# Reading the moving operand of the split products in pairs of columns from its two halves, in a one-core hybrid encoder layer

## The chip, the cores and the metric

The kernel runs on one NeuronCore of one Trainium2 chip. The metric is the device time of one execution in microseconds. A kernel is timed in several runs, and the median is given.

## The reference

One layer of a bidirectional encoder, on 1024 tokens of width 1024, in float32, followed by a final RMSNorm:

```
h = rmsnorm(x)
q, k, v, r, lr_f, lr_b, u, g_a, g_b = split(h @ w_in)
# branch A: gated linear attention, forward and backward, 4 heads, decays from lr_f and lr_b
o = gla(q, k, v, decay_f) + flipped gla(q, k, v, decay_b)
o = rmsnorm_per_head(o) * gla_norm * silu(r)
y_a = o @ w_branch_gla
# branch B: centred means over windows 2, 4, 8, 16, minus the token, a linear map per group
y_b = pooled(u) @ w_pool_group * pool_scale
x = x + (sigmoid(g_a) * y_a + sigmoid(g_b) * y_b) @ w_out
gate, up = split(rmsnorm(x) @ w_ffn_in)
x = x + (silu(gate) * up) @ w_ffn_out
return rmsnorm(x)
```

The feed-forward width is 2816. Nearly all of the arithmetic is in matrix products of float32 data.

## The kernel before

**The split products.** A float32 matrix is held as two parts of the type fp32r: the high part, a rounded copy that ScalarE makes (`split_to`, line 200), and the low part, the difference, that VectorE or GpSimd makes (line 201). A product of two such matrices is three matmuls into the same PSUM bank, high by high, high by low and low by high. `products` (line 270) issues them, at line 273. `mm3` (line 275) calls it and then `pump`, which advances a list of side tasks (splits, loads, evictions) by the cost of the product just issued, and so sets the order in which the other engines' instructions stand among the matmuls.

**A matmul** takes a stationary operand (128 rows by 128 columns, loaded into the array by a weight load of its own, LDWEIGHTS in the profile, on a row called PEld) and a moving operand (128 rows by up to 512 columns, in SBUF), and adds the result into a bank of 512 columns in PSUM. Each of the three matmuls of a product has a weight load of its own. Most split products move 512 columns. Those of the attention (tiles `kv` and `op`, 264 matmuls) move 256, the width of a head's values. All of them read neighbouring columns one after the other, and write them so.

**The stages.** The first norm and the projections of queries, keys, values and the gates r; the chunked attention of four heads, whose steps are interleaved with those projections; gates and pooling; the branch projection, the merge and the output projection; the second norm; the feed-forward product in, in 22 units of 128 rows of each half; and the product out. The large products from the gates on are done with Strassen's scheme in Winograd's form, seven products of half size with sums before and after. Sums and split weights that are needed later are stored to DRAM and loaded again.

**Four more places** issue matmuls of fp32r operands: `low_rank` (line 547), whose weights hold high and low parts side by side; the decays' map from rank 16 (line 822); and the identity products that add a residual into a bank at the end (line 2100). `products` is the fourth, through `mm3`, and directly for the attention's states (tile `kv`) and outputs (tile `op`). The scores (line 929), the products of queries with states (line 998) and all transposes work on plain fp32, and are not among them.

**What reads the banks.** ScalarE and VectorE read whole banks, or their first 256 columns, in the ordinary order, when the last matmul into them is done. Eight banks of PSUM are shared between two pools of three and five.

Of the kernel before, what the change touches and what calls it, by code (L numbers as in the profile page):

```python
# [53 lines left out]
def kernel(  # L54
# [20 lines left out]
    nc = tc.nc  # L75
# [21 lines left out]
    def slot(dtype=F32, shape=(2, HALF), s="slot"):  # L97
        return slots.tile([P, *shape], dtype, tag="slot", name=name(s))

    def t2(width=HALF, dtype=F32, s="t"):  # L100
        return tmp.tile([P, width], dtype, tag="t2", name=name(s), padded_shape=[P, HALF + 2 * PAD])
# [7 lines left out]
    def bank(pool, s="ps"):  # L109
        return pool.tile([P, HALF], F32, tag=pool.name, name=name(s))  # L110

    def as_f32(ap):
        return ap.bitcast(F32)
# [43 lines left out]
    def settle():  # L157
        while put_off:
            put_off.pop(0)[1]()

    def pump(dt):
        for entry in put_off:
            entry[0] -= dt
        while put_off and put_off[0][0] <= 0:
            put_off.pop(0)[1]()
        if pending:
            credit[0] += dt
            if credit[0] >= 2:
                credit[0] = 0.0
                pending.pop(0)()  # L170
        if aside:
            aside[0][1] -= dt

            if aside[0][1] <= 0 and not pending:
                cost = next(aside[0][0], None)
                if cost is None:
                    aside.pop(0)
                else:
                    aside[0][1] += cost
        if not side:  # L180
            return
        side[0][1] -= dt
        while side and side[0][1] <= 0:
            try:
                side[0][1] += next(side[0][0])
            except StopIteration:
                side.pop(0)
# [11 lines left out]
    def split_to(hi, lo, src, eng=nc.vector):  # L199
        nc.scalar.copy(hi, src)  # L200
        eng.tensor_tensor(lo, src, as_f32(hi), op=ALU.subtract)  # L201
# [65 lines left out]

    mm_banks = cycle([ps_mm])

    def products(ps, a, b, first=True, last=True, onto=False):  # L270

        for n, (i, j) in enumerate(((0, 0), (0, 1), (1, 0))):
            nc.tensor.matmul(ps, a[i], b[j], start=first and n == 0, stop=last and n == 2, skip_group_check=onto)  # L273

    def mm3(ps, a, b, first, last, onto=False):
        products(ps, a, b, first, last, onto)
# [19 lines left out]
    def feature_major(w, act, half, kts=KT):  # L296
        ps = bank(next(mm_banks))
        for k in range(kts):
            mm3(ps[:, :], w(k), act(k, half), k == 0, k == kts - 1)
        return ps  # L300
# [121 lines left out]
    up = slot(F32R, (HEADS, 2, DK), "up")  # L422
# [118 lines left out]
    lrT = slot(F32R, (2, HALF), "lrT")  # L541

    def low_rank(half):
        ps = bank(ps_mm)
        for k in range(KT):
            for i in range(2):
                nc.tensor.matmul(
                    ps[:, :], lw[k // 4][:, k % 4, :, :].rearrange("p a r -> p (a r)"), hT(k, half)[i],
                    start=k == 0 and i == 0, stop=k == KT - 1 and i == 1,
                )  # L550
            pump(2 / 3)
        nc.scalar.copy(lrT[:, half, :], ps[:, :])
        nc.vector.tensor_tensor(lrT[64:96, half, :], ps[64:96, :], as_f32(lrT[64:96, half, :]), op=ALU.subtract)
# [259 lines left out]
    def attention(h):  # L813
# [5 lines left out]
        zs, las = {}, {}  # L819
        for half, d in runs:  # L820
            z = bank(ps_g, "z")
            nc.tensor.matmul(z[:, :], up[:, h, d, :], lrT[:, half, :], start=True, stop=True)
            bias = b_dec[d][:, h : h + 1]
            la = t2(s="la")
            nc.vector.tensor_scalar(la[:, :], z[:, :], bias, 0.0, op0=ALU.add, op1=ALU.min)
            nc.scalar.activation(z[:, :], z[:, :], AF.Abs, bias=bias)
            zs[half, d] = z
            las[half, d] = la
            yield 1.3
# [94 lines left out]
        def scores(half):  # L924
            sc = [bank(ps_g, "sc") for _ in range(2)]
            for d in range(2):
                for i in range(4):
                    n = 4 * half + i
                    nc.tensor.matmul(
                        sc[d][:, i * CH : (i + 1) * CH], chunk_of(ke, n, d), chunk_of(qe, n, d),  # L930
                        start=True, stop=True,
                    )
            hi, lo = (t2(dtype=F32R, s="p")[:, :] for _ in range(2))
            nc.vector.copy_predicated(sc[1][:, :], keep.rearrange("p n c -> p (n c)"), sc[0][:, :])
            split_to(hi, lo, sc[1][:, :])
            return hi, lo
# [30 lines left out]
        for n in range(NT - 1, 0, -1):  # L967
            m = n - 1
# [9 lines left out]
        p = scores(0)  # L978
# [6 lines left out]
        for n in range(NT):  # L985
            half, i = n // 4, n % 4
# [22 lines left out]
            if n == 3:  # L1009
                p = q_next  # L1010
# [201 lines left out]
    for j in range(KT - 2):  # L1212
# [10 lines left out]
        for half in range(2):  # L1223
# [5 lines left out]
            ps = feature_major(w, hT, half)  # L1229
# [292 lines left out]
    for n, run in enumerate(gate_runs):  # L1522
        zs[n] = Gates(n)
        last = n == len(gate_units) - 1
# [387 lines left out]
    def load_piece():  # L1912
        if len(loaded_pieces) == len(pieces):
            return
        p, q, c = pieces[len(loaded_pieces)]
        g, w = slot(s="gor"), slot(s="wor")
        if p in RAW_B:
            i, j = RAW_B[p]
            src = w_ffn_out[(i * PAIRS + q) * P : (i * PAIRS + q + c) * P, j * HALF : (j + 1) * HALF]
            nc.sync.dma_start(w[:, :c, :], src.rearrange("(q p) c -> p q c", p=P))  # L1920
        else:
            nc.sync.dma_start(w[:, :c, :], t_out[p][:, q : q + c, :])
        nc.sync.dma_start(g[:, :c, :], g_out[p][:, q : q + c, :])
        loaded_pieces.append((w, g))

    def split_piece():
        n = len(ready_pieces)
        if n == len(pieces):
            return
        while len(loaded_pieces) <= n:  # L1930
            load_piece()
        c = pieces[n][2]
        both = []
        for src, eng in zip(loaded_pieces[n], (nc.vector, nc.gpsimd)):
            hi, lo = slot(F32R, s="oh"), slot(F32R, s="ol")
            split_to(hi[:, :c, :], lo[:, :c, :], src[:, :c, :], eng)
            both.append((hi, lo))
        ready_pieces.append(both)
# [42 lines left out]
    def load_x2():  # L1981
        t = len(x2)
        if t == NT:
            nc.sync.dma_start(gain_final[:, :], norm_final[None, :].broadcast_to([P, D]))
            return
        x2.append(slot(shape=(D,), s="x2"))
        nc.sync.dma_start(x2[t][:, :], x2_out[t])
# [76 lines left out]
    for at, p in enumerate(OUT_ORDER):  # L2064
        closing = at == len(OUT_ORDER) - 1
        if p in FIRST:
            banks[p in UP] = [bank(pool) for pool in (U_BANKS if p == 1 else X_BANKS)]
        sums = banks[p in UP]
        if closing:
            res, unit_matrix = slot(F32R, s="res"), slot(F32R, s="unit")[:, 0, :P]  # L2070
            residual = res[:, 0, :], res[:, 1, :]
            nc.scalar.copy(unit_matrix, ident[:, :])
            split_to(*residual, x2[NT - 1][:, COLS[0]])
        for i in range(CLOSE if closing else n_of):
            n = at * n_of + i
            while len(ready_pieces) <= n:
                split_piece()
            load_piece()
            if n < NT + 1:
                load_x2()  # L2080
            for m in range(4):
                piece_product(sums[m], n, m, i == 0 and p in FIRST, i == n_of - 1, p not in FIRST)
                if i == n_of - 1:
                    collect(p, m, sums[m][:, :])
                if m == (3 if i == n_of - 1 else 1):
                    split_piece()

                if m == 3 and n in (9, 10):
                    load_piece()
                    if n == 10:  # L2090
                        split_piece()
                if m == 3 and len(pieces) - n_of + CLOSE > n + 1 >= len(pieces) - 2 * CLOSE:
                    load_piece()
                    split_piece()
        if closing:
            settle()
            for m in range(4):
                if m == 3:
                    for part in residual:
                        nc.tensor.matmul(sums[m][:, :], unit_matrix, part, start=False, stop=False, skip_group_check=True)  # L2100
                for i in range(CLOSE, n_of):
                    piece_product(sums[m], at * n_of + i, m, False, i == n_of - 1, p not in FIRST)
                collect(p, m, sums[m][:, :])
# [29 lines left out]
```

## Time and profile before

| | us |
|---|---|
| median of 3 runs | 1374.78 |
| lowest and highest run | 1374.72, 1375.25 |
| profiled execution, first to last instruction (span) | 1373.4 |
| TensorE matmuls busy | 1361.4 |
| TensorE weight loads busy | 1132.9 |
| VectorE busy | 836.8 |
| GpSimd busy | 752.1 |
| ScalarE busy | 647.3 |

The span is that of one profiled execution, and the median that of the timed runs. They differ by 1.4 us, which is what lies around the first and the last instruction. Busy times are unions, so matmuls that overlap count once. The length of a single matmul in the profile reaches from its start to the end of its drain, and the next one starts before that end; how many fit into a stretch is read from the starts. Weight loads run beside the matmuls, on a row of their own (PEld). The granted clock of TensorE, as a mean over the span, was 0.999 of full speed.

### The profile page before, as it was taken

Reading aid. Unit: us, or ns where it says so; the run is one execution under the profiler, and the core shown is the slowest. Engines: PE = TensorE matmul, PEld = TensorE weight load, DVE = VectorE, ACT = ScalarE, POOL = GpSimd, SP = SyncE. Lnnn points to the kernel's source line nnn. Section 1 sums busy time; section 2 is a strip of 40 time slices with the busy share of each in tenths; the row PEclk is TensorE's granted clock in tenths of the full one; section 3 lists DMA queues with packets and bytes.
Section 4 is the critical chain, followed back from the end, with each engine's and each line's share of the span. In section 5 each row is a group of like instructions: output and inputs, shape, how many; then the busy total and the mean of one; then the engine's idle time right before and its main releaser. Section 6 shows DMA issues by size and latency. Waiting matters only on the chain. (4 is left out here: it accounts for less than half of the span.)

```text
span 1373.4 us, 17879 instructions
## 1 busy us (share of the span) xinstructions
PE 1361.4 (99%) x6310; PEld 1132.9 (82%) x6310; DVE 836.8 (61%) x1034; ACT 647.3 (47%) x1177; POOL 752.1 (55%) x557
## 2 busy tenths in 40 slices
PE   9999999999999999999999999999999999999998
PEld 7888888888888888888888888888888888888886
DVE  6974556554735777678883955655566556343375
ACT  7365666755534445554346533333333334444253
POOL 3323723222597547667764376666676667455454
PEclk9999999999999999999999999999999999999999
DMA  6321523314778569995416355555544447985451
GB/s 227 113 87 52 181 90 92 95 60 123 245 236 278 186 198 308 373 386 216 150 71 241 112 174 176 176 176 177 176 145 137 146 136 266 384 301 187 169 215 77
DMA packets 167834, 251.97 MB, mean 183 GB/s; under 512 B 11160, under 2 KB 94144, under 8 KB 167744
## 3 DMA queue, kind: packets, MB, share of 16 engines
q1 hardware_dynamic: 167600, 250.57, 53.8%
q8 instruction: 49, 0.80, 0.2%
q14 instruction: 41, 0.34, 0.1%
q10 hardware_dynamic: 144, 0.26, 0.0%
HBM read 168.74 MB, written 82.05 MB: 183 GB/s over the span
## 5 line engine op out<-in xcount | busy, mean ns | idle before, releaser
L201 POOL TENSOR_TENSOR wl<-fs,wh 128x512 fp32r<-128x512 f32 x124 | 173.1, 1400 | 163.5 <-ACT wh L200 104.0
L273 PE MATMUL ps<-gh,wh 128*128 128x512 f32 x616 | 240.5, 390 | 0.0
L273 PE MATMUL ps<-gl,wh 128*128 128x512 f32 x616 | 239.8, 389 | 0.3 <-DVE gl L1691 0.3
L273 PE MATMUL ps<-gh,wl 128*128 128x512 f32 x616 | 239.7, 389 | 0.0
L201 POOL TENSOR_TENSOR wl<-fraw,wh 128x512 fp32r<-128x512 f32 x93 | 134.0, 1442 | 75.0 <-ACT wh L200 72.4
L201 POOL TENSOR_TENSOR ol<-gor,oh 128x1024 fp32r<-128x1024 f32 (+1 forms) x42 | 101.3, 2417 | 86.0 <-ACT oh L200 71.7
L273 PE MATMUL ps<-hh,wh 128*128 128x512 f32 x356 | 145.1, 408 | 0.7 <-ACT ga L1474 0.7
L273 PE MATMUL ps<-hh,wl 128*128 128x512 f32 x356 | 139.0, 390 | 0.0
L273 PE MATMUL ps<-hl,wh 128*128 128x512 f32 x356 | 138.8, 390 | 0.0
L273 PEld LDWEIGHTS ps<-gl,wh 128*128 128x128 f32 x616 | 115.7, 188 | 24.5 <-DVE gl L1691 0.7
L273 PEld LDWEIGHTS ps<-gh,wh 128*128 128x128 f32 x616 | 115.7, 188 | 24.1 <-ACT hb L1710 0.2
L273 PEld LDWEIGHTS ps<-gh,wl 128*128 128x128 f32 x616 | 115.7, 188 | 23.9
L273 PE MATMUL ps<-oh,oh 128*128 128x512 f32 x308 | 119.8, 389 | 0.0
L273 PE MATMUL ps<-ol,oh 128*128 128x512 f32 x308 | 119.8, 389 | 0.0
L273 PE MATMUL ps<-oh,ol 128*128 128x512 f32 x308 | 119.8, 389 | 0.0
L201 POOL TENSOR_TENSOR wl<-wraw,wh 128x512 fp32r<-128x512 f32 x56 | 92.3, 1679 | 44.7 <-ACT wh L200 44.6
L201 POOL TENSOR_TENSOR wl<-raw,wh 128x512 fp32r<-128x512 f32 x34 | 47.4, 1404 | 108.3 <-ACT wh L200 71.9
L201 DVE TENSOR_TENSOR ol<-wor,oh 128x1024 fp32r<-128x1024 f32 (+1 forms) x42 | 62.8, 1506 | 68.1 <-ACT oh L200 55.5
L200 ACT CAST wh<-fs 128x512 fp32r<-128x512 f32 x124 | 76.1, 615 | 29.5 <-DVE fs L1093 28.3
L273 PEld LDWEIGHTS ps<-hh,wl 128*128 128x128 f32 x356 | 66.8, 188 | 14.4
L273 PEld LDWEIGHTS ps<-hh,wh 128*128 128x128 f32 x356 | 67.0, 188 | 13.1 <-ACT ga L1474 1.1
L273 PEld LDWEIGHTS ps<-hl,wh 128*128 128x128 f32 x356 | 67.0, 188 | 12.0
(281 smaller groups left out, 3073.4 us busy)
## 6 DMA issues: line engine op xcount, KB each, us to landing
fraw<-in_w_ffn_in_dram SPq DMA_DIRECT2D x44, 512.0 KB, 6.1
gor<-g_out SPq DMA_DIRECT2D x35, 512.0 KB, 6.1
fraw<-in_w_in_dram SPq DMA_DIRECT2D x22, 512.0 KB, 6.5
g_out<-s SPq DMA_DIRECT2D x44, 256.0 KB, 2.3
wor<-t_out SPq DMA_DIRECT2D x20, 512.0 KB, 3.7
raw<-in_w_in_dram SPq DMA_DIRECT2D x36, 256.0 KB, 5.1
g_out<-g SPq DMA_DIRECT2D x33, 256.0 KB, 2.6
x<-in_x_dram SPq DMA_DIRECT2D x16, 512.0 KB, 5.6
```

Of the source, the lines that this page charges most:

```text
L200: nc.scalar.copy(hi, src)
L201: eng.tensor_tensor(lo, src, as_f32(hi), op=ALU.subtract)
L273: nc.tensor.matmul(ps, a[i], b[j], start=first and n == 0, stop=last and n == 2, skip_group_check=onto)
```

## The change

Two helpers are added. `woven` takes an access pattern of `2 * 2 * c` columns as two halves, and walks through it in runs of two: columns 0 and 1 of the first half, columns 0 and 1 of the second, columns 2 and 3 of the first, and so on. `multiply` issues a matmul whose moving operand and whose output in PSUM are both walked through in that order. Every column still meets the same weights and ends at the same place of the bank. The stationary operand is passed as before. All matmuls of fp32r operands are issued through `multiply`; those of plain fp32 and the transposes stay as they were.

```
+    def woven(ap):
+
+        return ap.rearrange("p (a c e) -> p c a e", a=2, e=2)
+
+    def multiply(ps, a, b, **flags):
+        nc.tensor.matmul(woven(ps), a, woven(b), **flags)
+
     def products(ps, a, b, first=True, last=True, onto=False):
 
         for n, (i, j) in enumerate(((0, 0), (0, 1), (1, 0))):
-            nc.tensor.matmul(ps, a[i], b[j], start=first and n == 0, stop=last and n == 2, skip_group_check=onto)
+            multiply(ps, a[i], b[j], start=first and n == 0, stop=last and n == 2, skip_group_check=onto)
...
         for k in range(KT):
             for i in range(2):
-                nc.tensor.matmul(
+                multiply(
                     ps[:, :], lw[k // 4][:, k % 4, :, :].rearrange("p a r -> p (a r)"), hT(k, half)[i],
                     start=k == 0 and i == 0, stop=k == KT - 1 and i == 1,
                 )
...
             z = bank(ps_g, "z")
-            nc.tensor.matmul(z[:, :], up[:, h, d, :], lrT[:, half, :], start=True, stop=True)
+            multiply(z[:, :], up[:, h, d, :], lrT[:, half, :], start=True, stop=True)
...
                     for part in residual:
-                        nc.tensor.matmul(sums[m][:, :], unit_matrix, part, start=False, stop=False, skip_group_check=True)
+                        multiply(sums[m][:, :], unit_matrix, part, start=False, stop=False, skip_group_check=True)
```

## The prediction

> **What bounds the kernel now.** I read the page first: the engines' busy times, then the granted clock.
>
> ```profile
> span 1373.4 us, 17879 instructions
> PE 1361.4 (99%) x6310; PEld 1132.9 (82%) x6310; DVE 836.8 (61%) x1034; ACT 647.3 (47%) x1177; POOL 752.1 (55%) x557
> PEclk9999999999999999999999999999999999999999
> ```
>
> PE is busy for 99% of the span, nothing else is above 61% apart from its own weight loads, and the clock is granted nearly in full, so there is no throttle to lift or to fall into. Busy matmuls overlap, so I next read the chain of waits and the stretch that it names:
>
> ```profile
> 761.27 601.99 PE ps L273 x2654
> ```
>
> ```profile
> 761.00:1363.00 602.00, 601.73 (x2654) 498.27 (x2655) 339.45 (x327) 233.57 (x368) 366.72 (x234) 1.00 0.55 186
> ```
>
> The first row is one unbroken run on the path: 2654 products of line 273 in 601.99 us, 0.2268 us each. The second, busy time by stage (PE, PEld, DVE, ACT, POOL, then clock, DMA share, GB/s), says that in that stretch PE was idle for 0.3 us of 602. So the time is the number of matmuls times the spacing of their starts. The mean of about 389 ns that the groups show for one matmul includes its drain, which overlaps the next; the price is the spacing. It does not come from other traffic:
>
> ```profile
> 500.00:600.00 100.00, 100.00 (x441) 1.00 0.96 341
> ...
> 1000.00:1100.00 100.00, 100.00 (x443) 1.00 0.46 149
> ```
>
> With the DMA engines 96% busy or 46% busy, 100 us hold the same number of matmuls within two.
>
> **What the change touches.** It adds and removes no instruction, no wait, no tile, no DMA. It changes the order in which a product of fp32r operands reads its moving operand and writes its bank: columns 0, 1, 256, 257, 2, 3, 258, 259 and so on, for 512 columns. The stationary operand, loaded by its own instruction, is still read in order. How many products are touched is counted from the stage and group views:
>
> ```profile
> 0.00:1374.00 1374.00, 1313.74 (x5736) 1061.41 (x5736) 1.00 0.54 183
> ```
>
> ```profile
> L273 PE MATMUL kv<-vh,kt 128*128 128x256 f32 x112 | 33.7, 323 | 0.0
> ...
> L273 PE MATMUL op<-vh,p 128*128 128x256 f32 x64 | 17.1, 288 | 0.7 <-DVE p L201 0.4 <-ACT p L200 0.3
> ...
> L273 PE MATMUL kv<-vl,kt 128*128 128x256 f32 x56 | 15.7, 281 | 0.0
> ...
> L273 PE MATMUL op<-vl,p 128*128 128x256 f32 x32 | 9.0, 280 | 0.0
> L547 PE MATMUL ps<-hh,lw 128*128 128x512 f32 x16 | 6.4, 401 | 0.0
> ...
> L547 PE MATMUL ps<-hl,lw 128*128 128x512 f32 x16 | 6.3, 391 | 0.0
> L822 PE MATMUL z<-lrT,up 128*128 128x512 f32 x16 | 6.2, 390 | 0.0
> ...
> L2100 PE MATMUL ps<-res,unit 128*128 128x512 f32 x2 | 0.6, 389 | 0.0
> ```
>
> The first row is line 273 alone: 5736 matmuls. Of these 112 + 64 + 56 + 32 = 264 have 256 columns, so 5472 have 512. With 16 + 16 + 16 + 2 = 50 more from the other lines, 5522 matmuls of 512 columns and 264 of 256 are rewoven. The plain fp32 products and the transposes are not touched.
>
> **Where the spacing comes from.** Three stretches of the timeline (start, length, engine, line, what). First the settled case, then one around the attention's small products:
>
> ```profile
> 900.01 0.39 PE L273 MATMUL ps<-gh,wh 128*128 128x512 f32 x1
> ...
> 906.81 0.39 PE L273 MATMUL ps<-gh,wh 128*128 128x512 f32 x1
> ```
>
> ```profile
> 128.27 0.28 PE L273 MATMUL op<-vh,p 128*128 128x256 f32 x1
> 128.39 0.28 PE L273 MATMUL op<-vl,p 128*128 128x256 f32 x1
> 128.50 0.28 PE L273 MATMUL op<-vh,p 128*128 128x256 f32 x1
> 128.62 0.59 PE L998 MATMUL op<-sf,qe 128*128 128x256 f32 x2
> 128.87 0.58 PE L273 MATMUL ps<-hh,wh 128*128 128x512 f32 x1
> 129.28 0.39 PE L273 MATMUL ps<-hl,wh 128*128 128x512 f32 x1
> ...
> 131.59 0.39 PE L273 MATMUL ps<-hh,wh 128*128 128x512 f32 x1
> ```
>
> ```profile
> 900.01 0.19 PEld L273 LDWEIGHTS ps<-gl,wh 128*128 128x128 f32 x1
> 900.24 0.19 PEld L273 LDWEIGHTS ps<-gh,wl 128*128 128x128 f32 x1
> ```
>
> From 900.01 to 906.81 lie 30 spacings (the same product comes round after three): 6.80 / 30 = 0.2267 us for 512 columns. From 128.27 to 128.62 lie three of 256 columns: 0.35 / 3 = 0.117 us. The second 256 columns therefore cost 0.2267 - 0.117 = 0.110 us, which makes 0.219 us for 512 at the marginal rate and leaves a part of about 8 ns that every matmul pays whatever its width. From 129.28 to 131.59 ten spacings take 2.31 us, 0.231 each: after plain fp32 work has upset the rhythm, the same matmul takes 4 ns longer, then settles again. So the surplus is no constant fee; it depends on timing between two streams. The last fence shows which two I suspect: the next weight load starts together with each matmul and reads its 128 columns (0.19 us) while the matmul streams. The two L998 rows with the first product behind them take 129.28 - 128.62 = 0.66 us; less 0.231 for that product, each plain fp32 matmul takes 0.215 us for its 256 columns, with a weight load beside it as well. That is 0.84 ns per column, half the rate, so the moving stream asks for half as much.
>
> The Trainium skill speaks here, both ways. "TensorE: Matmul & The Clock Gate", section "Back-to-back issue gap", gives a 512-column matmul 215.8 ns at full clock; the rows above show 226.7, so about 11 ns here are above its figure, and a matmul brought down to it would make the estimate 1374.8 - 5522 x 0.0109 = 1315 us. The same page, "Step-by-step: what each phase is for", says that a weight load does not steal read bandwidth from the running matmul, since the two have ports of their own. By that rule my suspicion falls, and with it the gain: the time would be that of my first rival. The trace shows a surplus that comes once per matmul, and cannot show its cause.
>
> **The sum for the forecast.** I take the surplus to be collisions between the matmul's reads and the weight load's. Reading in order, the matmul walks through 512 / 0.227 = 2.26 columns per ns and the weight load through 128 / 0.19 = 0.67, so the one passes the other's place again and again. Reading pairs from two halves, each half advances at 1.13, nearer to the weight load's pace, and two streams that have stalled each other once can then stay out of each other's way for longer. No row shows a woven read, so I bound the cost.
> - Best end: nothing of the surplus is left, and 512 columns take the 0.215 us that I found for a plain fp32 matmul. 5522 x 0.0117 = 64.6 us, and as much a piece for the 264 is 3.1, unless they are bound by the weight load. Some 1307 to 1310 us.
> - Taken: the marginal rate of this very form, 0.219, that is 8 ns less per matmul, since it is the nearest row. (5522 + 264) x 0.008 = 46.3 us.
> - Other end of this case: a quarter of that, 2 ns, 11.6 us.
>
> Not all of it need arrive. Where PE is faster, what feeds it must be too, and one stage has no room:
>
> ```profile
> 540.00:560.00 20.00, 20.00 (x89) 1.00 1.02 347
> 560.00:580.00 20.00, 20.00 (x90) 1.00 1.00 378
> 580.00:600.00 20.00, 20.00 (x90) 1.00 1.03 409
> 600.00:620.00 20.00, 20.00 (x90) 1.00 0.95 361
> ```
>
> For 80 us the DMA engines are full (the share is the number before the last). PE would shorten this stage by 8 / 226.7 = 3.5%, 2.8 us, and the transfers can't; prefetch covers some of it. I charge 1 us, and 0 to 3 for the range. Elsewhere DVE, ACT and POOL are at 61% or less and gain nothing to wait for from 3.5%. 46.3 - 1 = 45 us off. The profiled execution's span is 1373.4 us, the median of the runs 1374.78, so 1.4 us lie around the span and stay: 1374.8 - 45 = **1330 us**.
>
> **The rivals.**
> - *Nothing changes.* The surplus belongs to this kind of matmul (a swap of weights, say) or is met by fetches too wide or too narrow to mind the order. For it: 0.2267 to the tenth of a nanosecond, over tiles that lie everywhere. Against: the 0.231 stretch. Time: 1374.8, within 0.2% (2.7 us, 0.5 ns per matmul; about what a measurement of this kernel can tell from no change).
> - *Slower: twice the fetches.* If the matmul fetches a group of neighbouring columns at once and keeps only the latest, pairs taken in turn from two halves fetch every group twice, and the weight load finds the memory taken twice as often. The 8 ns become 16: 0.235 us, and 5786 x 0.008 = 46 us on top, 1421. The unsettled stretch with 0.231 (+4.3 ns, 25 us, 1400) shows that such spacings occur. It decides as soon as one fetch serves more than two columns and is not kept. It ends on the other side at the same size as my forecast.
> - *Much slower: each jump costs a beat*, on the read or on the write into the bank. If a woven column takes the 0.84 ns of the plain fp32 rows, 512 take 0.430: 5522 x 0.203 + 264 x 0.098 = 1147 us, 2522 in all. For it: the bank is written in jumps too, in no matmul of this trace so far. The Trainium skill, "PSUM — Partial Sum Buffer", "Specifications (TRN2)", says of lines of 8 bytes that "any non-contiguous AP slows matmuls significantly", which would be this rival. But "Advanced Engine Details and Errata", "PSUM Cachelines", asks only that "Every two consecutive elements should be contiguous for best throughput", and "SBUF — State Buffer", "Door 1: The DMA port swizzle", asks two hits per line of 16 bytes; the pairs here keep both, and by those two the first rival comes out. No run here shows either.
>
> That the order is normalised away before it reaches the chip I hold for unlikely (the jumps can't be merged into one run) and count under the first rival.
>
> **How the numbers follow.** Forecast 0.47: the surplus is there, is paid once per matmul and moves with timing, so order can reach it. No change 0.25. Slower 0.28, of which 0.20 is the doubled fetch up to 1428 and 0.08 the much slower. The forecast's own range is 1308 (all of the surplus, no transfer late) to 1363 (2 ns each). With the two nearer rivals the range is 1308 to 1428 (the doubled fetch with another 7 us for unsettled stretches); the much slower case, and what of the doubling goes beyond, is left out. Faster 0.47, same 0.25, slower 0.28.
>
> **What would show it.** Right: 30 spacings in the stretch about 900 us take 6.55 us in place of 6.80, in every stage alike, and the run of L273 that ends the chain shrinks from 602 to about 581 us; the L998 and transpose rows stay as they are; PE stays at 98 to 99%, with at most 3 us of new idle time near 540 to 620. First rival: 6.80 and 602 again. Second: 6.9 to 7.1. Third: above 10. Wrong in the sum but not in the mechanism would be a shorter spacing with PE idle in its place behind late transfers or POOL's differences. Wrong in the mechanism would be 512-column and 256-column matmuls that gain in proportion to their width rather than the same each.

## The result, and the profile after

The changed kernel takes 1963.04 us (median of 4 runs, 1961.9 to 1963.34) against 1374.97 us for the kernel before (4 runs). The ratio is 1.4275, with a 95% interval of 1.4255 to 1.4295. That is 588 us slower, outside the predicted range and on the other side of the forecast.

The page of the changed kernel, the lines that answer to the first ones of before:

```profile
span 1961.3 us, 17898 instructions
PE 1951.4 (99%) x6310; PEld 1192.0 (61%) x6310; DVE 744.8 (38%) x1034; ACT 647.0 (33%) x1177; POOL 707.7 (36%) x557
PEclk9999999999999999999999999999999999999999
```

The same 6310 matmuls, at the same granted clock, still fill 99% of a span that is 43% longer. ScalarE's busy time is the same, VectorE's is 92 us shorter and GpSimd's 44; why those two are shorter stays open. PE's idle time is 9.9 us, against 12.0 before. So PE does not wait more; each matmul takes longer. The prediction said that the change adds no instruction; the trace has 19 more, all of them semaphore instructions, which aren't counted as busy. The run below that weaves the write alone has the same 17898 instructions and takes no longer than the kernel before. The chain of waits shows it in its longest piece (start, length, engine, line, count), and the stage view says that PE had no idle time within it:

```profile
1053.37 896.00 PE ps L275 x2688
```

```profile
1060.00:1940.00 880.00, 880.00 (x2642) 517.44 (x2641) 264.97 (x321) 226.30 (x359) 340.94 (x232) 1.00 0.38 127
```

896.00 / 2688 = 0.3333 us from one start to the next, against 0.2268 before: 106.5 ns more. All rewoven matmuls now stand under one line, and the stage view of that line alone counts them:

```profile
0.00:1962.00 1962.00, 1913.07 (x5786) 1122.94 (x5786) 1.00 0.39 128
```

5786 is the 5522 + 264 of the prediction. 5522 x 0.1065 = 588 us, the whole difference. That it fits so well is partly chance: the 264 narrow matmuls cost some more, and in the projections the spacing grows by less. Here is the timeline of such a stretch, first and last row of 21 spacings, and behind it one of narrow matmuls, first and last row of five:

```profile
182.88 0.51 PE L275 MATMUL ps<-hh,wh 128*128 128x512 f32 x1
...
189.77 0.51 PE L275 MATMUL ps<-hh,wh 128*128 128x512 f32 x1
```

```profile
151.09 0.34 PE L275 MATMUL op<-vh,p 128*128 128x256 f32 x1
...
151.92 0.35 PE L275 MATMUL kv<-vh,kt 128*128 128x256 f32 x1
```

6.89 / 21 = 0.328 us, where the prediction read 0.231 before; and 0.83 / 5 = 0.166 us for 256 columns, where it read 0.117. The narrow ones lose 49 ns and the wide ones 106.5, so the loss goes with the number of columns. The plain fp32 products, which were not rewoven, kept their mean length (379 ns before, 382 after):

```profile
L1005 PE MATMUL op<-sf,qe 128*128 128x256 f32 x56 | 16.8, 382 | 0.0
```

### The profile page after: what moved, and what is told of

Same layout as the page of the kernel before. It is cut to its first block, busy times and chain, and to the rows that moved or that the text cites. A ratio compares the mean times of both kernels' runs of the same rounds, so it can differ in the third digit from the quotient of the medians.

```text
span 1961.3 us, 17898 instructions
## 1 busy us (share of the span) xinstructions
PE 1951.4 (99%) x6310; PEld 1192.0 (61%) x6310; DVE 744.8 (38%) x1034; ACT 647.0 (33%) x1177; POOL 707.7 (36%) x557
## 4 chain that ended last, share of the span: by engine, by line
PE 99%; issue 0%; DMA 0%; DVE 0%; ACT 0%; POOLq 0%; POOL 0%; SPq 0%; DVEq 0%; ACTq 0%
PE ps L275 92%; PE kv L275 1%; PE op L1005 1%; PE op L275 1%; PE yb L275 1%; PE sc L936 1%; PE tr L333 0%; PE tp L1195 0%; PE kp L906 0%; PE tr L1714 0%; PE z L275 0%; DMA x<-in_x_dram 0%; DVE x L2000 0%; ACT sq L2035 0%; DVE xn L454 0%
## 5 line engine op out<-in xcount | busy, mean ns | idle before, releaser
L275 PE MATMUL ps<-gh,wh 128*128 128x512 f32 x616 | 312.9, 508 | 0.0
L275 PE MATMUL ps<-gh,wl 128*128 128x512 f32 x616 | 312.4, 507 | 0.0
L275 PE MATMUL ps<-gl,wh 128*128 128x512 f32 x616 | 312.4, 507 | 0.0
L275 PE MATMUL ps<-hh,wh 128*128 128x512 f32 x356 | 185.6, 521 | 0.7 <-ACT ga L1481 0.7
L275 PE MATMUL ps<-hh,wl 128*128 128x512 f32 x356 | 180.3, 507 | 0.0
L275 PE MATMUL ps<-hl,wh 128*128 128x512 f32 x356 | 180.3, 506 | 0.0
L275 PE MATMUL ps<-oh,oh 128*128 128x512 f32 x308 | 156.2, 507 | 0.0
L275 PE MATMUL ps<-ol,oh 128*128 128x512 f32 x308 | 156.2, 507 | 0.0
L275 PE MATMUL ps<-oh,ol 128*128 128x512 f32 x308 | 156.2, 507 | 0.0
L275 PE MATMUL ps<-trh,wh 128*128 128x512 f32 x176 | 89.2, 507 | 0.0
```

The source lines that it names most:

```text
L275: nc.tensor.matmul(woven(ps), a, woven(b), **flags)
```

## The experiments

In all of them the number that decides is the spacing of 512-column matmuls, worked out as length over count of the longest unbroken piece of line 275 (277 in one kernel) in the chain of waits. A time without an interval is that of a single run; runs of the kernel before beside them took 1374.6 to 1375.7 us. The edits are given against the changed kernel.

**Read or write.** The first two runs each keep one side of the change.

```
-        nc.tensor.matmul(woven(ps), a, woven(b), **flags)
+        nc.tensor.matmul(ps, a, woven(b), **flags)
```

> Only the moving operand is read woven, in runs of two; the bank is written in order, so its columns come out permuted and the output is not the reference's. Theory A (the jumps cost on the read): the spacing is the woven kernel's 333 ns and the time about 1963 us. Theory B (the jumps cost on the write into the bank): spacing 227 ns, time about 1375 us. Theory C (any pattern of three levels costs, on either side, the sides running in step): 333 ns and 1963 us here and in the run with the write alone. If read and write each cost a part, the two runs' surpluses over 1375 add up to 588 us.

Measured: 1962.91 us. The chain of the run with the read alone:

```profile
1053.25 896.00 PE ps L275 x2688
```

0.3333 us, to the last digit that of the full change.

```
-        nc.tensor.matmul(woven(ps), a, woven(b), **flags)
+        nc.tensor.matmul(woven(ps), a, b, **flags)
```

> Only the bank is written woven, in runs of two; the moving operand is read in order, so columns come out permuted and the output is not the reference's. Theory A (read): 227 ns and about 1375 us. Theory B (write): 333 ns and about 1963 us. Theory C (either side): 333 ns and about 1963 us.

Measured: 1374.66 us beside 1375.65 for the kernel before. The last run of the study took the same edit again, timed:

> The write alone woven, in pairs, the read in order (columns come out permuted, which changes what is computed), now timed against the kernel before. If the order of the write costs nothing: a ratio within 0.2% of 1. If a jump on the write has any price that the read's had hidden, even a hundredth of the read's 106 ns per matmul: 6 us, a ratio of 1.004.

Measured: 1375.05 us (10 runs) against 1374.92 (13 runs), ratio 1.000, interval 0.9991 to 1.001. Its chain:

```profile
761.10 602.00 PE ps L275 x2654
```

0.2268 us. Theory A holds: all of the 588 us is in the order of the read, and the order of the write costs nothing that can be measured.

**How long the runs are.** Runs of four and of eight, both sides woven. A piece, from here on, is a group of 16 bytes, that is four neighbouring columns of 4 bytes:

```
-        return ap.rearrange("p (a c e) -> p c a e", a=2, e=2)
+        return ap.rearrange("p (a c e) -> p c a e", a=2, e=4)
```

> Both sides woven, but in runs of four columns: 128 runs in place of 256 per 512 columns. If each jump costs a fixed time (the surplus of 106.7 ns over 256 runs is 0.42 ns per run), the spacing is 226.7 + 128 x 0.42 = 280 ns and the time about 1669 us. If what costs is a piece of 16 bytes that is used by half, runs of four use whole pieces: 227 ns, about 1375 us. If the pattern's three levels cost as such, 333 ns.

> Both sides woven in runs of eight columns, 64 runs per 512 columns. Fixed time per jump: 226.7 + 64 x 0.42 = 253 ns, about 1522 us. Half-used pieces of 16 bytes: 227 ns, about 1375 us. Three levels as such: 333 ns, 1963 us.

Measured: 1498.41 us for fours (the run with `e=8`: 1460.68). The chains, fours and then eights:

```profile
814.12 672.01 PE ps L275 x2688
```

```profile
794.47 654.09 PE ps L275 x2688
```

0.2500 and 0.2433 us. None of the three theories hit. A fixed price per jump is refuted: from 256 jumps to 128 the surplus falls from 106 to 23 ns, from 128 to 64 only to 17. Most of the price vanishes where a run fills 16 bytes; a rest stays.

**Forward, without the two halves.** The same walk through one stretch, with every second run left out on the first pass:

```
-        return ap.rearrange("p (a c e) -> p c a e", a=2, e=2)
+        return ap.rearrange("p (a c e) -> p c a e", c=2, e=2)
```

> Runs of two on both sides, but walked forward with every second pair left out, then the pairs left out: columns 0, 1, 4, 5, 8, 9 and so on, then 2, 3, 6, 7. No jump between halves; every pair lies 16 bytes behind the one before. If a half-used piece of 16 bytes is what costs, the spacing is 333 ns and the time 1963 us as with the two halves. If what costs is the leap between two distant places, about 227 to 250 ns, 1375 to 1500 us.

> Runs of four on both sides, walked forward with every second run left out, then the runs left out: columns 0 to 3, 8 to 11 and so on. Whole pieces of 16 bytes, no leap between halves. If the 23 ns that runs of four from two halves cost above 227 come from the leap between halves, the spacing is 227 ns and the time 1375 us. If any break of the forward order costs, 250 ns and 1498 us as with the halves.

Measured: 2636.41 us for pairs, 1397.65 for fours (`e=4`). The chains:

```profile
1408.15 1212.60 PE ps L275 x2688
```

```profile
772.04 613.66 PE ps L275 x2654
```

The timeline of the first, with the weights and the moving operand of each matmul, shows the same from start to start, 0.45 us, with nothing between:

```profile
1500.00 0.63 PE L275 MATMUL ps<-gh,wh 128*128 128x512 f32 x1
1500.45 0.63 PE L275 MATMUL ps<-gl,wh 128*128 128x512 f32 x1
1500.90 0.63 PE L275 MATMUL ps<-gh,wl 128*128 128x512 f32 x1
1501.35 0.63 PE L275 MATMUL ps<-gh,wh 128*128 128x512 f32 x1
```

Pairs 16 bytes apart take 0.4511 us, which is worse than the change itself and above both forecasts; fours take 0.2312, near the first of theirs. So jumping between halves is not what costs the pairs their time. Per piece of 16 bytes that is visited: before, 226.8 / 128 = 1.77 ns; pairs forward, which visit every piece twice, far apart in time, 451.1 / 256 = 1.76 ns; fours forward, 231.2 / 128 = 1.81 ns. A piece costs the same whether two or four of its columns are used.

A wider distance, `c=4`, in pairs:

> Both sides in pairs walked forward 32 bytes apart, in four passes; all columns are read once and the product is the same. 256 fetches, none of a neighbouring piece. If the 1.76 ns of the pairs 16 bytes apart are the price of a neighbour and other distances take the 1.30 ns of the halves: 333 ns, 1963 us. If every forward fetch takes 1.76 ns: 451 ns, 2636 us. If a fetch brings 32 bytes and more, so that distance adds fetches: above 451.

Measured: 2686.47 us.

```profile
1434.16 1236.49 PE ps L275 x2688
```

0.4600 us, 1.80 ns per visit: the distance hardly matters. This run also fixes the size of a piece. If a fetch brought 8 bytes, pairs 16 bytes apart would have cost no more than reading in order. If it brought 32, those pairs would find every second place already fetched, and pairs 32 bytes apart would take twice as long as they. Both took about the same, and twice the order of before; so a piece is 16 bytes.

**Whose surplus it is.** The prediction had put the 8 to 11 ns that the kernel before spends above the column time down to collisions with the weight load. Two runs on the order of before:

```
-        nc.tensor.matmul(woven(ps), a, woven(b), **flags)
+        nc.tensor.matmul(ps, a[:, 0:1].broadcast_to([P, P]), b, **flags)
```

> The order of before on the moving side and in the bank; the stationary operand of every fp32r product is its first column 128 times over, so that a weight load reads one place (this changes what is computed). The prediction's theory, that the 8 to 11 ns above the column time are collisions of the matmul's reads with the weight load's walk through its columns: the spacing falls to 216 to 219 ns and the time to 1315 to 1330 us, or at least changes. Rival, a fee of this kind of matmul or of its own reads: 226.7 ns and 1375 us.

Measured: 1394.58 us, slower than before.

```profile
767.49 615.13 PE ps L275 x2654
```

0.2318 us. The surplus did not go; it grew by 5 ns. Where the weight load reads does have a hold on the spacing, but its walk through the columns is not the cause of the surplus.

```
-        nc.tensor.matmul(woven(ps), a, woven(b), **flags)
+        nc.tensor.matmul(ps, a, b[:, 0:4].unsqueeze(1).broadcast_to([P, ps.shape[-1] // 4, 4]), **flags)
```

> The order of before in the bank and in the weights; the moving operand is its first four columns over and over (this changes what is computed), so that the matmul reads one piece of 16 bytes and never leaves it. If the 8 to 11 ns above the column time come from the moving operand's fetches of new pieces, alone or against the weight load's: 216 to 219 ns, 1315 to 1330 us. If they are a fee per matmul: 226.7 ns, 1375 us.

Measured: 1323.67 us.

```profile
757.26 355.11 PE ps L275 x1644
```

The timeline, three rows that come round every 0.65 us:

```profile
899.82 0.38 PE L275 MATMUL ps<-gh,wh 128*128 128x512 f32 x1
900.03 0.38 PE L275 MATMUL ps<-gl,wh 128*128 128x512 f32 x1
900.25 0.38 PE L275 MATMUL ps<-gh,wl 128*128 128x512 f32 x1
```

0.2160 us. The surplus is gone when the moving operand never leaves one piece, with the weight loads as before. So it belongs to the fetches of new pieces by the moving operand: 512 columns take 0.216 us, 0.42 ns each, and four of them 1.69 ns, while in order a new piece came only every 1.77. It is also what the Trainium skill's formula for a single matmul's gap gives at this size ("TensorE: Matmul & The Clock Gate", "Back-to-back issue gap", 215.8 ns at full clock); here the figure holds once the reads keep up.

The stretch of 0.231 us that the prediction read behind the plain fp32 products is gone too. In the same place of this run, first and last row of ten spacings:

```profile
125.41 0.38 PE L275 MATMUL ps<-hl,wh 128*128 128x512 f32 x1
...
127.56 0.38 PE L275 MATMUL ps<-hh,wh 128*128 128x512 f32 x1
```

2.15 / 10 = 0.215 us. One rival is left. No run is without weight loads, so a loss that they cause at the moving fetches wherever they read isn't excluded by these two runs. The pairs walked forward speak against it:

```profile
1500.00:2500.00 1000.00, 1000.00 (x2218) 460.44 (x2217) 192.95 (x257) 183.69 (x287) 295.57 (x202) 1.00 0.29 98
```

Weight loads (the second of the busy times) stand beside 46% of PE's time there, against 83% in the stretch that the prediction shows, and a piece costs 1.76 ns against 1.77.

**Is every change of piece a fetch?** Three loops over places that were just read, moving side alone:

```
-        nc.tensor.matmul(woven(ps), a, woven(b), **flags)
+        nc.tensor.matmul(ps, a, b.rearrange("p (a c e) -> p c a e", a=2, e=2)[:, 0:1, :, :].broadcast_to([P, ps.shape[-1] // 4, 2, 2]), **flags)
```

> Moving side alone: columns 0, 1, 256, 257 over and over (this changes what is computed), bank written in order. The jumps of the woven kernel without its progress: 256 changes between two pieces of 16 bytes, never a new one. Theory P (every change of piece is a fetch, whether the piece was just read or not; a far one takes 333 / 256 = 1.30 ns): 333 ns, about 1963 us. Theory Q (the last pieces are kept, only a new piece is a fetch): 216 ns, about 1324 us, as with one piece.

Measured: 1331.09 us. The next run takes its two pairs from `b[:, 0:8]`, 16 bytes apart, the third repeats `b[:, 0:8]` whole:

> As the run before, but with columns 0, 1, 4, 5 over and over: two neighbouring pieces of 16 bytes (this changes what is computed). Theory P, with a fetch of a neighbouring piece at 451 / 256 = 1.76 ns: 451 ns, about 2636 us. Theory P with one price per change: 333 ns, 1963 us. Theory Q: 216 ns, 1324 us.

> Moving side alone: columns 0 to 7 over and over (this changes what is computed): two neighbouring pieces, each read whole, 128 changes as in the order of before, never a new piece. Theory P: 128 x 1.77 ns = 227 ns, about 1375 us. Theory Q: 216 ns, about 1324 us.

Measured: 1326.30 and 1325.50 us. The chains of the three:

```profile
760.08 358.31 PE ps L275 x1644
```

```profile
758.08 356.48 PE ps L275 x1644
```

```profile
758.20 555.62 PE ps L275 x2565
```

0.2180, 0.2168 and 0.2166 us. Theory P falls and theory Q holds: 256 jumps per matmul over 1024 bytes cost 2 ns in all when the two places stay the same. Of what was tried so far, only a place that is new costs much.

**How many places are held.** This leads to a theory of the changed kernel's 333 ns, called R. Per eight columns it makes two first visits, at 1.77 ns each, in which only two columns are used, and two returns, which take just their columns' time, 2 x 0.42 ns. 64 x (2 x 1.77 + 2 x 0.84) = 334 ns. With `a=4`, four quarters in turn, a return comes after three other pieces:

> Both sides woven in pairs from four quarters in turn: each piece of 16 bytes is returned to after three others. Theory R (a first visit takes 4.25 columns' time, 1.77 ns; a return to a piece still held takes its two columns' time, 0.83 ns): if four pieces are held, as with two halves, 128 x (1.77 + 0.83) = 333 ns and about 1963 us. If only two are held, every visit is a first one: 256 x 1.77 = 453 ns, about 2640 us.

Measured: 2592.3 us.

```profile
1385.07 1191.69 PE ps L275 x2688
```

0.4433 us, that is 1.73 ns for each of 256 visits: 2% below the second figure of the forecast: a return after three others costs as much as a first visit. Two places are held, four are not; three were not tried.

**The weight load's share in the woven read.**

```
-        nc.tensor.matmul(woven(ps), a, woven(b), **flags)
+        nc.tensor.matmul(ps, a[:, 0:1].broadcast_to([P, P]), woven(b), **flags)
```

> The woven read in pairs, bank written in order, and the stationary operand its first column 128 times (this changes what is computed). If the woven 333 ns are the matmul's own reads (first visits at 1.77 ns, returns at 0.83): 328 to 338 ns, 1940 to 1990 us. If collisions with the weight load's walk make a good part of the 106 ns: clearly below, under 300 ns and 1780 us.

Measured: 1933.8 us.

```profile
1042.14 878.09 PE ps L275 x2688
```

0.3267 us, 6.7 ns less than 333.3 and just below the forecast of 328 to 338. With the weight load's walk taken away from both orders, the woven read still costs 326.7 - 231.8 = 95 ns more than the read in order, of 106.5 with it. So about nine tenths of the loss don't hang on where the weight load reads.

**The rest that fours and eights keep.** Fours from two halves fetch each piece once, and by R should take 227 ns. They take 250. Two runs, moving side alone: fours with the same weight column, and fours from two places 252 columns apart:

```
+    def apart(ap):
+
+        n = ap.shape[-1] // 2
+        (step, count), _ = ap.ap
+        return bass.AP(tensor=ap.tensor, offset=ap.offset, ap=[[step, count], [4, n // 4], [n - 4, 2], [1, 4]])
...
-        nc.tensor.matmul(woven(ps), a, woven(b), **flags)
+        nc.tensor.matmul(ps, a, apart(b), **flags)
```

> Moving side alone in runs of four from two halves, and the stationary operand its first column 128 times (this changes what is computed). If the 23 ns of runs of four from two halves are collisions with the weight load's walk: the spacing falls from 250 ns towards 227 to 231 ns, 1375 to 1395 us. If they belong to the two halves: 250 ns, about 1498 us.

> Moving side alone in runs of four from two places 252 columns apart in place of 256, which are 1008 bytes in place of 1024 (four columns are read twice and four not at all, which changes what is computed). If the 23 ns come from two places that lie a power of two apart: 227 to 232 ns, 1375 to 1400 us. If any second place costs them: 250 ns, about 1498 us.

Measured: 1489.98 and 1460.69 us. The chains:

```profile
809.79 667.94 PE ps L275 x2688
```

```profile
794.44 654.09 PE ps L277 x2688
```

0.2485 and 0.2433 us. Where the weight load reads accounts for 1.5 of the 23 ns, the distance of exactly 1024 bytes for 6.7. The other 15 or so stay open, if the two may be added; 4 of them appear without a second stream too, in the fours walked forward (231.2). A first visit takes 1.90 to 1.95 ns in runs of four and eight from two halves, in place of 1.77. With 1.95, R would give 128 x (1.95 + 0.84) = 357 ns for the changed kernel. So R is good to about a tenth, and that its 334 meets the measured 333.3 so closely is partly luck.

## Why the prediction was wrong

*That PE's spacing is the time* was right. The longest piece of the chain is one unbroken run of `products` in both kernels, and matmuls counted times the change of spacing gives the measured difference.

*The count of the rewoven matmuls*, 5522 and 264, was right.

*That the change costs nothing elsewhere* was right: PE's idle time did not grow, and the write into the bank costs nothing (ratio 1.000, 0.9991 to 1.001). I had counted that write as a reason for the much slower rival. The measurement sides with the sentence of the Trainium skill that I quoted from "Advanced Engine Details and Errata", "PSUM Cachelines": two neighbouring elements at a time suffice. I was wrong that this section asks only that, for the line above it there says the same as "PSUM — Partial Sum Buffer", "Specifications (TRN2)", that any non-contiguous pattern slows matmuls, and this does not hold for pairs.

*The step that failed* is the one between the surplus and the gain: "I take the surplus to be collisions between the matmul's reads and the weight load's", and from it "two streams that have stalled each other once can then stay out of each other's way for longer". The surplus was there, 10.8 ns a matmul where I had taken 8: without new pieces the same matmul takes 0.216 us and the kernel 1324 us. That this lies six below the forecast is luck, for the bigger gain and a bigger loss to idle time (below) cancel. But the surplus comes with the moving operand's new pieces, and weaving adds to it. A new piece comes every 1.77 ns, and reading in order uses four columns from it, 1.69 ns of work. The order of before is thus the one that just about keeps up, with 5% missing; pairs use two columns at a visit, and the spacing went from 226.8 to 333.3 ns where I had 219. I read the 231 ns stretch as evidence for collisions; it goes to 215 with the moving operand in one piece, the weight loads as before. Where the weight load reads does move the spacing by some 5 to 7 ns (with the weight column fixed, 226.8 became 231.8 and 333.3 became 326.7). The Trainium skill's rule in "TensorE: Matmul & The Clock Gate", "Step-by-step: what each phase is for", that a weight load steals nothing, thus holds but for those few ns, as far as runs can tell that all have weight loads. Why the one order got slower by it and the other faster stays open.

*The split of 0.2267 into 8 ns per matmul and a rate per column* was what led there. It came from the 0.117 us of the 256-column matmuls, which stand in short groups among plain fp32 products, where the 512-column ones too were off their settled spacing. The surplus is better put per piece: 128 x 0.08 ns = 10 ns per 512 columns. By the prediction's own sign, a gain or loss in proportion to the width, the mechanism was wrong: weaving cost 49 ns at 256 columns and 106.5 at 512.

*The rival with the doubled fetch* had the group of neighbouring columns right, and missed twice. The two groups read last are kept: a return costs no fetch. And it priced a fetch at its collisions, 8 ns more per matmul, where the price is a visit that lasts longer than its columns' work: a first visit takes 1.77 ns and gives two columns, 0.84 ns of work, so 0.93 ns are lost 128 times, 119 ns, less the 10 that were lost before: 109, measured 106.5. *The much slower rival* had a side, but its price, 0.84 ns for every column, is that of pairs that are never returned to: 0.430 us and 2522 predicted, where pairs forward measured 0.451 us and 2636, and quarters 0.443 and 2592. That this lies so near is chance, for the 0.84 came from another kind of matmul. Half of the visits in the changed kernel are returns, so it lands between.

*The two hits per line of 16 bytes* that I took from the Trainium skill ("SBUF — State Buffer", "Door 1: The DMA port swizzle") as enough for full rate were the reason to give this case 0.08. The 16 bytes are borne out by the pairs 16 and 32 bytes apart. That two hits suffice is not, for this read: two of four columns used per visit cost 333 to 460 ns against 227. The same passage says that each access that crosses to a new line pays a penalty; I left that out, and the pairs cross twice as often as the order of before.

*Late transfers.* With a longer spacing they could not show. The run with one moving piece is the test: by its spacing, 5522 x 0.0108 = 60 us and some 2 us for the narrow ones should have gone, to 1313 us; it measured 1323.67. Its PE line against that of before (1373.4 - 1361.4 = 12.0 us idle):

```profile
span 1322.0 us, 17879 instructions
PE 1301.2 (98%) x6310; PEld 1137.2 (86%) x6310; DVE 838.4 (63%) x1034; ACT 644.9 (49%) x1177; POOL 751.3 (57%) x557
```

20.8 us of idle time, 9 more. The stage view of that run (PE busy, clock, DMA share) says where; in the kernel before, PE's idle time in the same four slices was 0.9, 0.2, 0.0 and 0.2 us:

```profile
100.00:200.00 100.00, 97.57 (x540) 1.00 0.34 110
200.00:300.00 100.00, 98.34 (x547) 1.00 0.28 86
...
500.00:600.00 100.00, 99.31 (x459) 1.00 1.00 369
600.00:700.00 100.00, 97.75 (x459) 1.00 0.44 151
```

The full DMA stage that I had named, now 500 to 600, loses 0.7 us. More goes in the attention before it, where the DMA share is a third, and after it. PE's waits there are many and short, on VectorE, GpSimd and ScalarE in turn:

```profile
PE ps L275 <- POOL wl L201: 2.6, 3, 1.4
...
PE kv L275 <- DVE st L918: 1.2, 1, 1.2
PE tr L1714 <- ACT xn L1781: 1.1, 1, 1.1
PE kv L275 <- DVE kt L201: 0.9, 2, 0.6
```

So "Elsewhere DVE, ACT and POOL are at 61% or less and gain nothing to wait for" was wrong too: means over the span hide places where a result arrives just in time. I had charged 1 us, with 3 as the end; of some 62 us, 11 were lost, 9 of them as idle time.

## What to carry to other kernels

Where matmuls stand back to back, the order in which the moving operand is read has a price. For the fp32r matmuls of this kernel it can be added up visit by visit: a first visit to a piece of 16 bytes takes 1.77 ns whether two or four of its columns are used, and a return to one of the two pieces read last takes 0.42 ns per column. The sum is off by up to a tenth when two streams are read in turn (227 for 250 ns in runs of four). With such operands keep the read in order; the bank's write may be walked in pairs for nothing. A surplus over the column time is best tested by taking each stream's progress away, one at a time, before a cure is built on a guess at its cause.

## What the runs showed of the hardware that was not expected

- A matmul of 512 fp32r columns read in order is held up by its moving operand's fetches: 226.8 ns, against 216.0 when the read stays in one piece.
- Two pieces of 16 bytes are held at once, 1024 bytes apart too (218.0 ns for 256 alternations); after three others a return costs as much as a first visit (443.3 ns).
- Fetching from two streams in turn takes longer than from one (250.0 and 243.3 ns for whole pieces, against 226.8), and a distance of 1008 bytes takes 6.7 ns less than 1024.
- Weights that are all one column make an in-order matmul slower by 5 ns and a woven one faster by 6.7.
